# Opening of an attention with a scan beside it: the scan's kernels loaded in quarters and reordered on GpSimd, context chunks copied on the chip, the second unit's preparation not put ahead

## The chip, the cores and the metric

The kernel runs on 1 core of a Trainium2 chip. The metric is device time in microseconds of one execution; 3074.2 us is the median of 3 runs of the kernel before.

## The reference

Two layers of a transformer-like block over 1024 latent tokens and 256 context tokens, width 1024, all in fp32. Each layer first mixes tokens with four head groups that read one input projection and write one output projection, then applies a squared-ReLU MLP:

```
z  = modulate(rms_norm(x, g_pre_mix), sh1, sc1) @ w_in          # zc the same for the context
oa = gqa_mixer(z, zc, ...)     # A: grouped-query attention, 4 heads, 2 key heads, latent + context keys
ob = s5_mixer(z, zc, ...)      # B: bidirectional diagonal state-space scan, 16 groups x 16 channels, 64 states
on = na_mixer(z, zc, ...)      # C: 2-D neighbourhood attention, 4 heads
od = fourier_mixer(z, ...)     # D: 2-D DFT, then a linear map
y  = concatenate([oa, ob, on, od]) @ w_out
x  = x + g1 * rms_norm(y, g_post_mix)
x  = x + g2 * rms_norm(sq_relu_mlp(modulate(rms_norm(x, g_pre_mlp), sh2, sc2), w_mlp1, w_mlp2), g_post_mlp)
```

The context is carried through the first layer only (it is read but not updated in the second). For this change B matters: for each of 16 groups and both directions, a linear recurrence over 1280 positions, started for the latent part from the context's final states:

```
hc = linear_scan(einsum('blgh,gph->blgp', uc_g, bbar), abar, None, reverse)
h0 = hc[:, 0] if reverse else hc[:, -1]
h  = linear_scan(einsum('blgh,gph->blgp', u_g, bbar), abar, h0, reverse)
y  = y + einsum('blgp,ghp->blgh', h, cmat).real.reshape(b, n, S5_CH)
```

## The kernel before

The program is unrolled Python, run once, on one core. It goes layer by layer through stages: first norm, input projection, attention, output projection, MLP. Products that must be exact in fp32 are made of three products of a high and a low part. A planner, which works with a timing model when the program is built, takes what the Python code emits with its dependencies and gives each engine a fixed order: among instructions that it believes ready, the one emitted earliest goes first. An engine then runs its list strictly in order and waits in front of an instruction whose inputs are not there. What is emitted under `early(gen, n)` (L143) counts as emitted n instructions earlier. SP issues the loads and stores, in order as well.

The attention stage (`attention`, L827) works through units: with j one of two key heads and b a block of queries, first the grouped-query units (in layer 0: j0b0, j0b1, j0b2, j1b0, j1b1, j1b2, where b2 are the context's queries; in layer 1 without b2), then four heads of neighbourhood attention. Three streams run beside each other. The main of unit i (`gqa_main`, L629) goes through 10 key tiles in two steps each: scores on TensorE (L653), an exponential on ScalarE (L654), two steps later the products with the values (L622). The preparation of unit i+1 (`gqa_prep`, L555) is woven in three steps to one step of the main, under `early` with 600: the queries are split and transposed (L522, copies at L149), then come 16 reductions of score tiles (products L586, VectorE L588) and 4 of the context's (L593, L595), whose results are transposed into the second query tile. The preparation of unit 0 runs beside the end of the input projection. The scan (`s5_scan`, L1259) is the third stream, one step to two steps of the main.

The scan works in chunks of 8 positions: 128 chunks of latents and 32 of context, so that u, the tile s5u, holds for a partition (position in the chunk, channel) and each of 16 groups 192 columns: 32 context chunks, 128 latent chunks, and the context again, as the two directions need it. `s5_load` (L1250) fills it with 16 loads from HBM: for each of the 8 positions one of 160 columns (L1256) and one of the 32 context columns (L1257). The tile tm (s5tm) holds for each group the 128x128 matrix that carries the inside of a chunk. It comes from HBM as t0 (s5t), all 16 groups by 8 loads at once (L1334), and four times, behind group 1, 5, 9 and 13 in the code, four groups of it are reordered into tm by ScalarE (L1345, recorded at the helper's line L149). For each group, `front` (L1288) multiplies u by v (product L1290), rotates by cs and sn on VectorE with a swap of halves by ScalarE, scans, multiplies on GpSimd (L155), swaps again on ScalarE and adds on GpSimd; `rear` (L1318), two groups later, makes the output from tm (L1321) and from the scan's result (L1323) and stores it. The loads of v, cs and sn (L1284) are issued one group ahead, with two buffers.

Of the kernel before, what the change touches and what calls it, by code (L numbers as in the profile page):

```python
# [11 lines left out]
F32 = mybir.dt.float32  # L12
# [20 lines left out]
class K:  # L33
# [795 lines left out]
    def attention(self, l, st, o, fnet):  # L829


        units = st["units"]
        ng = sum(u["kind"] == "g" for u in units)
        ctx = any(u.get("b") == 2 for u in units)
        up = self.open(f"up{l}")
        for n, w, b in (("on", 512, 2), ("onn", TOK, 1), ("rt", 10, 2)):
            up.tile([128, w], F32, tag=n, bufs=b, name=n)
        pg = self.open(f"attG{l}")
        st["fp"], st["pg"] = up, pg
        pc = self.open(f"attC{l}", "right")  # L840
        st["k"].append(self.keys(pc, "g1"))
        st["q"].append(self.queries(pc, "g1", 1024))
        if ctx:
            st["q"].append(self.queries(pc, "gc", 512))
        sp = self.open(f"s5{l}")
        side, every = self.s5_scan(sp, l), 2
        self.ps_open("A", 2, "AM")
        for i, u in enumerate(units):
            ahead = [] if u.get("b") == 2 else [i + 1]
            if i + 1 < len(units) and units[i + 1].get("b") == 2:  # L850
                ahead.append(i + 2)
            ahead = [k for k in ahead if k < len(units)]
            if sp is not None and any(units[k]["kind"] == "n" for k in ahead):

                for _ in side:
                    pass
                sp.release()
                sp = None
                pn = st["pn"] = self.open(f"attN{l}")
                st["n"] = [self.na_set(pn, 0)]  # L860
            if i == ng:
                for p in (pc, st["pb"], st["zp"]):
                    p.release()
                pa = self.open(f"attO{l}")
                st["n"].append(self.na_set(pa, 1))
                self.ps_open("A", 2, "A")
                self.ps_open("M")
                side, every = fnet, 5 / 2
            main = self.gqa_main(st, u, o) if u["kind"] == "g" else self.na_main(st, u, o)
            main = self.along(main, st.get("fin", iter(())))  # L870
            main = self.every(main, side, every)
            self.weave(main, self.early(itertools.chain(*(self.attn_prep(st, k) for k in ahead)), 600), 3)
        for _ in st["fin"]:
            pass
        for _ in fnet:
            pass
        for p in (pa, pn, pg, up):
            p.release()
# [371 lines left out]
    def s5_load(self, u, l):  # L1250

        nc = self.nc
        us = self.u5D[l].rearrange("(g h) j c -> j h g c", h=16)
        for j in range(8):
            js = slice(j * 16, (j + 1) * 16)
            nc.sync.dma_start(u[js, :, 32:192], us[j])  # L1256
            nc.sync.dma_start(u[js, :, 0:32], us[j][:, :, 128:160])  # L1257

    def s5_scan(self, p, l):  # L1259

        nc = self.nc
        dr = self.s5D[l]
        u = p.tile([128, 16, 192], F32, name="s5u")
        self.s5_load(u, l)
        r8 = p.tile([128, 32], F32, name="r8")
        nc.sync.dma_start(r8, dr["r8"])
        tm = p.tile([128, 16, 128], F32, name="s5tm")

        def swap(dst, src):

            for a in (0, 64):
                self.copy(dst[a:a + 64], src[64 - a:128 - a])


        zs = [p.tile([128, 2, 160], F32, name=f"z{i}") for i in range(3)]
        for z in zs:
            nc.vector.memset(z[:, 0, 128:129], 0.0)
            nc.vector.memset(z[:, 1, 159:160], 0.0)

        def ins(g):  # L1280

            ts = [p.tile([128, 2, w], F32, tag=n, bufs=2, name=n) for n, w in (("v", 128), ("cs", 160), ("sn", 160))]
            for t, n in zip(ts, ("v", "cs", "sn")):
                nc.sync.dma_start(t, dr[n][:, g])  # L1284
            return ts

        def front(g, v, cs, sn):
            pv = self.ps1()[:, :320].rearrange("p (d c) -> p d c", d=2)  # L1288
            for d in range(2):
                nc.tensor.matmul(pv[:, d], v[:, d, :], u[:, g, 32 * d:32 * d + 160], start=True, stop=True)  # L1290
            m1, m2, m3 = (p.tile([128, 2, 160], F32, tag=n, bufs=2, name=n) for n in ("m1", "m2", "m3"))
            self.tt(m2, pv, sn, OP.mult)
            self.tt(m1, pv, cs, OP.mult)
            swap(m3, m2)
            self.tt(m1, m1, m3, OP.subtract)
            gg = p.tile([128, 2, 160], F32, tag="gg", bufs=2, name="gg")
            for d in range(2):
                y, x = gg[:, d, :], m1[:, d, :]
                if d:
                    y, x = y[:, ::-1], x[:, ::-1]  # L1300
                k = d * 16 + g
                nc.vector.tensor_tensor_scan(y, r8[:, k:k + 1].to_broadcast([128, 160]), x, 0.0, op0=OP.mult, op1=OP.add)
            z1, z2 = (p.tile([128, 2, 160], F32, tag=n, bufs=2, name=n) for n in ("g1", "g2"))
            self.tt(z1, gg, sn, OP.mult, nc.gpsimd)
            swap(z2, z1)
            self.tt(gg, gg, cs, OP.mult)
            z = zs[g % 3]

            for d, c0, c1, n in ((0, 0, 31, 128), (0, 129, 0, 31), (1, 0, 1, 159)):
                self.tt(z[:, d, c0:c0 + n], gg[:, d, c1:c1 + n], z2[:, d, c1:c1 + n], OP.add, nc.gpsimd)  # L1310
            return z

        def outs(g):

            x = p.tile([128, 2, 128], F32, tag="x1", bufs=2, name="x1")
            nc.sync.dma_start(x, dr["x"][:, g])
            return x

        def rear(g, z, x):
            py = self.ps1()[:, :160]  # L1320
            nc.tensor.matmul(py, tm[:, g, :], u[:, g, 32:192], start=True, stop=False)  # L1321
            for d in range(2):
                nc.tensor.matmul(py, x[:, d, :], z[:, d, :], start=False, stop=d == 1)  # L1323
            y = p.tile([128, 160], F32, tag="y", bufs=2, name="y")
            self.copy(y, py)
            nc.sync.dma_start(dr["y"][g], y)

        before, xs = [], []
        tabs = ins(0)
        yield  # L1330

        t0 = p.tile([128, 16, 128], F32, name="s5t0")
        for j in range(8):
            nc.sync.dma_start(t0[j * 16:(j + 1) * 16], dr["e"][:, :, (7 - j) * 16:(7 - j) * 16 + 128])  # L1334
        yield
        yield
        for g in range(16):
            now, tabs = tabs, ins(g + 1) if g < 15 else None
            st = (g, front(g, *now))
            if g < 2:  # L1340
                xs.append(outs(g))
            if g % 4 == 1:

                gs = slice(g - 1, g + 3)
                self.copy(tm[:, gs].rearrange("p g (h j) -> p g j h", j=8), t0[:, gs].rearrange("p g (j h) -> p g j h", j=8))  # L1345
            yield
            before.append(st)
            if len(before) > 2:
                rear(*before.pop(0), xs.pop(0))
                xs.append(outs(g))  # L1350
                yield
        for st in before:
            rear(*st, xs.pop(0))
            yield
# [490 lines left out]
```

## Time and profile before

| | |
|---|---|
| median of 3 runs (lowest, highest) | 3074.2 us (3071.66, 3086.07) |
| profiled execution | 3064.83 us |
| its span, first to last instruction | 3062.3 us |
| mean granted TensorE clock | 0.972 of full |
| busy: TensorE, VectorE, ScalarE, GpSimd | 2920.0, 1632.1, 1084.1, 901.7 us |
| first attention begins about, second about | 303 us, 1936 us |

All readings are of one profiled execution; times are from the start of its span. Instructions of the program's queues run in order on each engine, so an engine's idle time in front of an instruction names what it waited for. PE is TensorE, DVE VectorE, ACT ScalarE, POOL GpSimd, SPq the queue of SP that issues loads and stores. A shared helper has one line for all its uses: L149 is every copy by ScalarE, L155 every two-input operation, L522 every transpose of this kind.

### The profile page before, as it was taken

How to read it: one execution, taken by the hardware profiler on the slowest of the kernel's cores; microseconds unless marked ns; L12 is line 12 of the kernel's file. 1: busy time of each engine (PE TensorE's matmuls, PEld its weight loads, DVE VectorE, ACT ScalarE, POOL GpSimd, SP SyncE). 2: the span in 40 equal slices, each digit the busy share in tenths (PEclk: the TensorE clock that was granted, in tenths of full speed). 3: DMA queues.
4: the chain of work that ended last, by engine and by line, in shares of the span. 5: the costliest groups of instructions: out<-in, count | busy, mean ns of one | idle time of the engine just before them, and what ended most of it. 6: DMA issues, size and time to landing. Idle time of an engine off the chain costs nothing. (4 is left out here: it accounts for less than half of the span.)

```text
span 3062.3 us, 41885 instructions
## 1 busy us (share of the span) xinstructions
PE 2920.0 (95%) x16492; PEld 2539.9 (83%) x16492; DVE 1632.1 (53%) x2245; ACT 1084.1 (35%) x1858; POOL 901.7 (29%) x849
## 2 busy tenths in 40 slices
PE   6999899999999999999999899898999999999998
PEld 3798798887888889898988788798887888888887
DVE  3465565664775544754554776465755333343334
ACT  3444554553422222422222344365543322121212
POOL 1464123225421122512112564022224111111113
PEclk8999798999999999999999999899999999999999
DMA  7533525342543322532333443525343111111113
GB/s 271 185 117 113 89 80 137 113 145 99 174 140 128 128 82 83 171 112 97 117 104 104 160 122 123 78 81 154 108 145 124 43 54 56 42 49 48 56 42 110
DMA packets 237077, 335.36 MB, mean 110 GB/s; under 512 B 46705, under 2 KB 182993, under 8 KB 236881
## 3 DMA queue, kind: packets, MB, share of 16 engines
q1 hardware_dynamic: 236880, 332.70, 35.6%
q8 instruction: 129, 2.11, 0.3%
q14 instruction: 68, 0.55, 0.1%
HBM read 279.06 MB, written 53.54 MB: 109 GB/s over the span
## 5 line engine op out<-in xcount | busy, mean ns | idle before, releaser
L161 PE MATMUL ps<-mh,wh 128*128 128x320 f32 (+1 forms) x1536 | 518.8, 338 | 11.9 <-DVE y L155 6.8
L149 ACT ACTIVATE wh<-raw 128x1024 fp32r<-128x1024 f32 x234 | 243.0, 1057 | 791.2 <-PE ps L163 551.6
L163 PE MATMUL ps<-mh,wl 128*128 128x320 f32 (+1 forms) x1536 | 517.1, 337 | 0.6 <-DVE wl L152 0.6
L162 PE MATMUL ps<-ml,wh 128*128 128x320 f32 (+1 forms) x1536 | 516.9, 337 | 0.0
L161 PE MATMUL ps<-wh,hidh 128*128 128x512 f32 x1152 | 452.3, 393 | 2.2 <-DVE y L155 2.0
L163 PE MATMUL ps<-wh,hidl 128*128 128x512 f32 x1152 | 448.3, 390 | 3.1 <-POOL hidl L152 3.1
L162 PE MATMUL ps<-wl,hidh 128*128 128x512 f32 x1152 | 450.0, 391 | 0.0
L155 DVE TENSOR_TENSOR y<-ps,y 128x1024 f32<-128x1024 f32 (+1 forms) x253 | 306.7, 1218 | 262.1 <-PE ps L163 261.8
L152 POOL TENSOR_TENSOR hidl<-r,hidh 128x640 fp32r<-128x640 f32 (+1 forms) x128 | 189.1, 1477 | 675.6 <-DVE r L155 656.5
L152 DVE TENSOR_TENSOR wl<-raw,wh 128x1024 fp32r<-128x1024 f32 x188 | 286.2, 1532 | 170.7 <-ACT wh L149 163.8
L161 PEld LDWEIGHTS ps<-mh,wh 128*128 128x128 f32 x1536 | 289.8, 189 | 37.5 <-issue 7.3
L163 PEld LDWEIGHTS ps<-mh,wl 128*128 128x128 f32 x1536 | 289.5, 189 | 21.2 <-DVE wl L152 1.2
L162 PEld LDWEIGHTS ps<-ml,wh 128*128 128x128 f32 x1536 | 289.7, 189 | 20.9
L161 PEld LDWEIGHTS ps<-wh,hidh 128*128 128x128 f32 x1152 | 217.2, 189 | 53.7 <-issue 6.2
L163 PEld LDWEIGHTS ps<-wh,hidl 128*128 128x128 f32 x1152 | 216.9, 188 | 49.2 <-POOL hidl L152 3.5
L152 POOL TENSOR_TENSOR wl<-raw,wh 128x1024 fp32r<-128x1024 f32 x48 | 117.2, 2442 | 472.4 <-ACT wh L149 472.1
L162 PEld LDWEIGHTS ps<-wl,hidh 128*128 128x128 f32 x1152 | 217.1, 188 | 43.3
L155 DVE TENSOR_TENSOR r<-r 128x640 f32<-128x640 f32 (+1 forms) x128 | 98.9, 773 | 241.9 <-ACT hidh L1511 241.4
L1509 ACT ACTIVATE r<-ps 128x640 f32<-128x640 f32 (+1 forms) x128 | 82.3, 645 | 366.7 <-PE ps L163 359.9
L622 PEld LDWEIGHTS ps<-zg,e 128*128 128x128 f32 x1312 | 186.1, 199 | 15.8 <-ACT e L654 0.8
L622 PE MATMUL ps<-zg,e 128*128 128x65 f32 x1312 | 179.1, 273 | 0.4 <-ACT e L654 0.4
L294 DVE SCALAR_TENSOR_TENSOR acc<-raw,cst,acc 128x1024 f32<-128x1024 f32 x70 | 101.5, 1474 | 137.3 <-DMA raw<-in_w_ada_dram 137.3
(433 smaller groups left out, 5431.3 us busy)
## 6 DMA issues: line engine op xcount, KB each, us to landing
raw<-in_w_mlp_dram SPq DMA_DIRECT2D x192, 512.0 KB
raw<-in_w_ada_dram SPq DMA_DIRECT2D x96, 512.0 KB
raw<-in_w_in_dram SPq DMA_DIRECT2D x28, 512.0 KB
x<-x SPq DMA_DIRECT2D x26, 512.0 KB
x<-h SPq DMA_DIRECT2D x18, 512.0 KB
x<-in_x_dram SPq DMA_DIRECT2D x16, 512.0 KB
raw<-in_w_out_dram SPq DMA_DIRECT2D x16, 512.0 KB
bq<-in_na_bq_dram SPq DMA_DIRECT2D x8, 800.0 KB
```

Of the source, the lines that this page charges most:

```text
L149: self.nc.scalar.activation(out, in_, AF.Copy, scale=scale)
L152: (eng or self.nc.vector).tensor_tensor(out=out, in0=a, in1=b, op=OP.subtract)
L155: (eng or self.nc.vector).tensor_tensor(out=out, in0=a, in1=b, op=op)
L161: self.nc.tensor.matmul(ps, ah, bh, start=start and i == 0, stop=False)
L162: self.nc.tensor.matmul(ps, ah, bl, start=False, stop=False)
L163: self.nc.tensor.matmul(ps, al, bh, start=False, stop=stop and i == n - 1)
L294: nc.vector.scalar_tensor_tensor(acc[c], x, col, acc[c], op0=OP.mult, op1=OP.add)
L622: self.nc.tensor.matmul(po[:, b * 512 + c * 65:b * 512 + c * 65 + 65], e, vf[:, kt, :], start=False, stop=(b, c) in end)
L1509: nc.scalar.activation(r.rearrange("p (b n) -> p b n", b=nb), ps[:, :nb, :w], AF.Relu)
```

## The change

The context's second place in u is no longer loaded: after the 8 loads GpSimd copies columns 160 to 191 of all groups to columns 0 to 31. The tile t0 shrinks from 16 groups to 4, with two buffers. A new inner function `kernels(g0)` issues the 8 loads for four groups and lets GpSimd reorder them into tm; it is called behind the front of groups 0, 4, 8 and 12, where before all loads stood ahead of group 0 and ScalarE reordered behind groups 1, 5, 9 and 13. While unit 0 runs, the preparation of unit 1 counts as emitted 40 instructions earlier in place of 600; for all later units 600 stays.

```diff
-            self.weave(main, self.early(itertools.chain(*(self.attn_prep(st, k) for k in ahead)), 600), 3)
+            self.weave(main, self.early(itertools.chain(*(self.attn_prep(st, k) for k in ahead)), 600 if i else 40), 3)
...
             nc.sync.dma_start(u[js, :, 32:192], us[j])
-            nc.sync.dma_start(u[js, :, 0:32], us[j][:, :, 128:160])
+
+        nc.gpsimd.tensor_copy(u[:, :, 0:32], u[:, :, 160:192])
...
-        t0 = p.tile([128, 16, 128], F32, name="s5t0")
-        for j in range(8):
-            nc.sync.dma_start(t0[j * 16:(j + 1) * 16], dr["e"][:, :, (7 - j) * 16:(7 - j) * 16 + 128])
+        def kernels(g0):
+
+            t0 = p.tile([128, 4, 128], F32, tag="s5t0", bufs=2, name="s5t0")
+            gs = slice(g0, g0 + 4)
+            for j in range(8):
+                nc.sync.dma_start(t0[j * 16:(j + 1) * 16], dr["e"][:, gs, (7 - j) * 16:(7 - j) * 16 + 128])
+            nc.gpsimd.tensor_copy(tm[:, gs].rearrange("p g (h j) -> p g j h", j=8), t0.rearrange("p g (j h) -> p g j h", j=8))
+
...
-            if g % 4 == 1:
-
-                gs = slice(g - 1, g + 3)
-                self.copy(tm[:, gs].rearrange("p g (h j) -> p g j h", j=8), t0[:, gs].rearrange("p g (j h) -> p g j h", j=8))
+            if g % 4 == 0:
+                kernels(g)
```

## Rows read from the trace of the kernel before

**Rows 1.** The page's busy times: us, share of the span, instructions.
```profile
PE 2920.0 (95%) x16492; PEld 2539.9 (83%) x16492; DVE 1632.1 (53%) x2245; ACT 1084.1 (35%) x1858; POOL 901.7 (29%) x849
```
**Rows 2.** Stretches: length, busy us (instructions) by engine, clock, DMA share, GB/s.
```profile
326.70:334.40 7.70, 0.02 (x1) 0.00 (x0) 0.90 (x2) 4.31 (x6) 0.00 (x0) 0.64 0.64 117
334.40:342.60 8.20, 8.16 (x29) 7.20 (x30) 2.67 (x4) 1.74 (x4) 0.00 (x0) 0.51 0.01 2
...
350.00:470.00 120.00, 118.39 (x871) 109.45 (x871) 79.58 (x162) 79.33 (x165) 37.52 (x71) 1.00 0.28 81
...
1959.30:1969.40 10.10, 0.00 (x0) 0.00 (x0) 1.43 (x3) 4.30 (x6) 0.00 (x0) 0.72 0.59 99
1969.40:1976.60 7.20, 7.16 (x28) 6.68 (x29) 1.47 (x3) 1.67 (x3) 0.00 (x0) 0.50 0.00 0
```
**Rows 3.** Timeline, layer 0: start, us, engine, line, operation [idle before <-releaser].
```profile
330.09 3.87 ACT L149 ACTIVATE s5tm<-s5t 128x512 f32<-128x512 f32 x4 [10.63 <-DMA cs<-s5cs]
...
334.44 1.22 PE L653 MATMUL ps<-g0q,g0k 128*128 128x512 f32 x2 [7.72 <-ACT e L654]
```
**Rows 4.** Timeline, layer 1, the same place.
```profile
1965.10 3.87 ACT L149 ACTIVATE s5tm<-s5t 128x512 f32<-128x512 f32 x4 [10.43 <-DMA v<-s5v]
...
1969.44 1.22 PE L653 MATMUL ps<-g0q,g0k 128*128 128x512 f32 x2 [10.16 <-ACT e L654]
```
**Rows 5.** Stretches around the openings and at the change of attention, columns as before.
```profile
304.00:314.00 10.00, 7.22 (x27) 4.28 (x26) 7.89 (x14) 1.62 (x3) 2.32 (x2) 0.72 1.22 148
314.00:326.00 12.00, 11.54 (x42) 9.33 (x41) 5.29 (x9) 4.28 (x7) 0.00 (x0) 0.53 1.23 140
...
326.00:328.00 2.00, 0.72 (x4) 0.37 (x3) 1.29 (x2) 0.00 (x0) 0.00 (x0) 1.00 1.23 129
...
470.00:560.00 90.00, 82.01 (x552) 74.40 (x551) 52.55 (x106) 42.81 (x83) 26.25 (x27) 0.89 0.66 165
...
2090.00:2180.00 90.00, 81.36 (x564) 72.93 (x563) 53.09 (x109) 42.46 (x81) 26.98 (x32) 0.92 0.61 156
```
**Rows 6.** Groups by form: busy us, mean ns | idle before. GpSimd's, then ScalarE's.
```profile
L182 POOL CAST wh<-raw 128x1024 fp32r<-128x1024 f32 x2 | 2.1, 1037 | 25.8 <-DMA raw<-in_w_out_dram 25.8
...
L152 POOL TENSOR_TENSOR wl<-tab,wh 128x512 fp32r<-128x512 f32 x4 | 5.2, 1288 | 15.2 <-ACT wh L149 15.2
...
L149 ACT ACTIVATE g1q<-ps 128x512 fp32r<-128x512 f32 x8 | 4.6, 599 | 3.9 <-DMA uf<-cst__3248 3.5 <-PE ps L522 0.3
L149 ACT ACTIVATE s5tm<-s5t 128x512 f32<-128x512 f32 x4 | 3.9, 1120 | 10.6 <-DMA cs<-s5cs 10.6
```
**Rows 7.** Timeline, layer 0: the scan's first work on TensorE and on GpSimd.
```profile
349.36 0.76 PE L1290 MATMUL ps<-s5u,v 128*128 128x160 f32 x4
...
353.30 0.88 POOL L155 TENSOR_TENSOR g<-gg,sn 128x320 f32<-128x320 f32 x1 [43.10 <-DVE ql L155]
...
358.67 0.49 PE L1321 MATMUL ps<-s5u,s5tm 128*128 128x160 f32 x2
```
**Rows 8.** SP's queue, layer 0: issues in order of time, then its longest wait.
```profile
311.25 0.34 SPq L1257 DMA_DIRECT2D s5u<-u  x1
...
313.09 0.33 SPq L1257 DMA_DIRECT2D s5u<-u  x1
...
318.42 5.29 SPq L1334 DMA_DIRECT2D s5t<-s5e  x8
...
SPq L1284 <- PE ps L593: 22.1, 1, 22.1
```
**Rows 9.** The second unit: reductions (ns min/median/max), last query copies, first scores, longest wait.
```profile
L588 DVE TENSOR_REDUCE nm<-ps x61: 658/685/693, 292.3 to 440.3; 128x1 f32<-128x512 f32 x61
...
355.68 1.08 ACT L149 ACTIVATE g1q<-ps 128x512 fp32r<-128x512 f32 x2
...
367.79 0.71 PE L653 MATMUL ps<-g1q,g0k 128*128 128x512 f32 x2
...
373.92 0.73 PE L653 MATMUL ps<-g1q,g0k 128*128 128x512 f32 x2 [1.47 <-ACT e L654]
```

## The prediction

> **What bounds the kernel now.** I read the page's busy times and slices first, then a table of stretches, then the engines in order of time where TensorE stood still, then the queue of SP. The profiled execution took 3064.8 us, of which 3062.3 are the span; the median of the three runs shown is 3074.2, so it lies 9.4 us below, and I carry its differences over to the median.
>
> TensorE is busy 95% of the span, so the idle 5% (some 142 us) and the stretches at a low clock are all that a reordering can win [rows 1]. Two of its gaps lie just behind the opening of the two attentions, and in both its busy time is practically zero: 326.7 to 334.4 and 1959.3 to 1969.4 us [rows 2]. Behind them attention is bound by TensorE: from 350 to 470 us it works 118.4 of 120 us at full clock while VectorE and ScalarE have 80 each [rows 2].
>
> What ends the gap is read in order of time. In the first layer ScalarE stands idle for 10.63 us, from 319.5, does four copies s5tm<-s5t in one go, and only then the next exponentials; TensorE goes on at 334.44, released by an exponential after 7.72 us of idling [rows 3]. The second layer repeats it: 10.43 us of waiting, the same four copies, 10.16 us of idle TensorE [rows 4]. The trace names the cs or v load as releaser; those loads stand behind the s5t load in SP's queue, and the copies' only input is s5t, so I take the wait as that on the s5t load (all 16 groups, 1 MB) landing. ScalarE works strictly in order, so the next exponentials stand behind copies that nobody needs for long: the first product with s5tm comes at 358.67 [rows 7].
>
> The gap costs twice. TensorE's clock is at half (the 0.50 level, 1.2 GHz) in 334.4 to 342.6 and in 1969.4 to 1976.6 [rows 2], so what ran there took double. Before the first gap the clock had come back to full (1.00 in 326 to 328 [rows 5]), so it is the gap that threw it down again.
>
> **The change, part by part.**
>
> *Reorder off ScalarE.* The four copies of 1120 ns per layer leave ScalarE, and with them its wait for the load. What goes: 7.72 us in the first layer and 10.16 in the second. Without the gap the clock stays up, and 8.2 us and 7.2 us of half-clock work would take half: 4.1 and 3.6 us. Sum 7.7 + 10.2 + 4.1 + 3.6 = 25.6 us. The bounds: nothing, if another wait takes its place; 25.6 plus the small idle pieces just before (0.46 of 12 us in 314 to 326 [rows 5], taken for both layers), 26.5. Next late would be the exponentials themselves, which follow at TensorE's pace. I take all of 25.6, since TensorE stays the busiest engine behind it and what starts earlier there ends earlier.
>
> *The reorder on GpSimd.* Five new instructions a layer: four reorders and one plain copy, each 128x512. The trace has no such reorder on GpSimd. Below: half the 1037 ns of its plain 128x1024 conversion, 0.52 us. Above: its two-input 128x512, 1.29 us. On ScalarE the reorder costs 1120 against 599 ns for a plain copy of that size [rows 6]; that ratio on 0.52 gives 0.97, and I take 1.0. Five microseconds a layer are hidden while GpSimd does nothing: its first scan multiply at 353.30 comes after 43 us of idleness [rows 7]. Should the cover go, a late multiply holds the swaps on ScalarE and behind them the exponentials. The Trainium skill (GPSIMD Engine Reference, Performance pitfalls for Q7 kernels) gives 1.9 cycles an element, 2.9 for wide strides on the read; at its 1.2 GHz an estimate of 0.8 to 1.2 us, inside these bounds, so the sum stays; no run here has shown it yet.
>
> *Context chunks copied on the chip.* Eight loads of 32 KB a layer go, in runs of 128 bytes (32 values). SP issues one pair of loads, 192 KB, each 1.84 us there (from 311.25 to 313.09 [rows 8], and so in the pairs before). If bytes set the pace, the pair without its sixth takes 1.53; if packets do, half, 0.92. The eight end 2.4 to 7.3 us earlier. The copy needs the last of the eight loads, as the first product on s5u did, and adds 0.5 to 1.3 us. That product runs at 349.36, some 36 us after the last load was issued [rows 7, 8], or some 24 with the 11.8 us of the first layer gone: worth nothing by itself, costs nothing. The Trainium skill (DMA: Bandwidth & Descriptors, Specifications) states 512 bytes as the least transfer at line rate; by it the 7.3 is nearer. The rows only bracket it; it moves the second rival, not the sum.
>
> *The load in quarters.* 32 issues in place of 8, less the 8 chunk loads: 16 more a layer on SP. Eight whole ones took 5.29 us to issue, 0.66 each [rows 8], an upper bound; the cheapest there took 0.33: 5 to 11 us. Two buffers make the third quarter wait for the first reorder; behind it stand the next groups' v, cs and sn loads. SP has cover: it then waited 22.1 us for TensorE [rows 8]. Cost 0; if the cover is gone, some of the 11 us reach the third group's products, behind which there is other work for TensorE.
>
> *Second unit not put ahead.* Its 20 reductions (0.69 each, 13.8 us on VectorE) were done before its last query copies, which end at 356.8, and its first scores began at 367.79: 11 us of slack [rows 9]. Interleaved three steps to one of the first unit, its 23 steps are traced by the 8th of some 21, so they keep most of it. At that boundary TensorE idled 1.47 us [rows 9]. I charge as much again per layer, 3.0 us; bounds 0 and the 23.4 us a layer of the third rival.
>
> Sum: -25.6 + 3.0 = -22.6 us: 3042.2 on the profiled execution, 3051.6 on the median, so **3052**. Its own range is 3044 to 3059 (26.5 won and a little luck; 15.4 left). With 0.5% (15.4 us) as what a measurement tells from no change, that is faster.
>
> **Rivals.**
> 1. *Forecast*: both gaps go, about -22. Chance 0.55.
> 2. *The wait moves.* The planner that fixed each engine's order put the copies where it believed the load landed, some 10 us before it did. It can do so again: the first scan product drawn into TensorE's waits of 304 to 314 (7.2 of 10 us busy [rows 5]) and standing there for the chunk copy; or GpSimd standing before a quarter, the scan multiply behind it, then swaps and exponentials. For: GpSimd, idle, invites it, and the last s5u load, issued at 313.09 [rows 8], moves only to 306 to 311 and lands later. Against: a quarter lands before the whole, and higher-priority work stood before the scan. Price: 4 to 10 us back per layer, so -22.6 + 8 to 20: 3060 to 3072, middle 3066, mostly no change. Chance 0.23.
> 3. *The second unit is late (slower).* At the first boundary TensorE waits for the whole preparation: 13.8 us of reductions, two query copies of 0.6 [rows 6], and a clock like that behind the first unit's own preparation, 0.72 for 10 and 0.53 for 12 us [rows 5], which is 8.4 us lost: 23.4 a layer, 47 in all, less the 25.6, +21: 3095. It decides from 12.8 us a layer, that is from about half of that left over at the boundary. For: the third unit's preparation keeps its 600 and now ranks before it. Against: the slack above, and that unit's queries go into the buffer which the first unit still reads. Chance 0.12.
> 4. *More than the sum.* The scan's earlier start also fills the weak stretch at the change to the second kind of attention (82.0 of 90 us busy in 470 to 560, 81.4 in 2090 to 2180 [rows 5]); half of those 16.6 us: -31, 3043. Chance 0.10.
>
> That the change does nothing of what it says is in the second, with the wait merely on another engine.
>
> **How the numbers follow.** Faster by over 0.5%: most of the forecast (0.49), all of the fourth (0.10), a little of the second (0.03): 0.62. Slower: most of the third, 0.10, and 0.02 of the second: 0.12. Same: 0.26. The range leaves out the third and the tail of the fourth: 3036 to 3078.
>
> **What would show it.** Right: no ScalarE copies s5tm; exponentials following each other with under 4 us between them from 317 and 1946 on; no TensorE gap over 2 us until the first boundary; full clock from about 326 and 1951 on; the reorders on GpSimd at about 1 us. Wrong: TensorE waiting before L1290 or GpSimd's multiplies waiting on DMA (second), a gap and half clock at the first scores of the second unit (third), or attention shorter by 25 us and the time lost again behind it.

## The result, and the profile after

The changed kernel takes 3041.24 us (median of 5 executions, 3037.68 to 3051.14), against 3074.2 us before (3063.73 to 3086.07): a ratio of 0.9891, 95% interval [0.9862, 0.9919], 33 us. It is faster, as forecast; the forecast was 3052 us with a range of its own from 3044 to 3059, so the median lies 3 us under that. The profiled execution took 3037.68 us, 3035.5 of them the span.

The page's busy times, in the columns of [rows 1]: the work has hardly changed, TensorE's share of a shorter span has risen.

```profile
PE 2916.6 (96%) x16492; PEld 2538.7 (84%) x16492; DVE 1635.7 (54%) x2245; ACT 1078.5 (36%) x1850; POOL 912.6 (30%) x859
```

Stretches of the kernel after, in the columns of [rows 2]: the places of the two former gaps, the stretch from 350 us on, the boundary to the second unit, and the second layer's opening.

```profile
320.00:330.00 10.00, 10.00 (x39) 8.38 (x39) 4.97 (x8) 3.70 (x6) 1.73 (x2) 0.56 0.57 150
330.00:340.00 10.00, 10.00 (x70) 9.15 (x70) 5.85 (x9) 3.45 (x6) 3.49 (x3) 1.00 0.24 51
350.00:470.00 120.00, 117.97 (x833) 108.61 (x832) 74.05 (x148) 75.75 (x157) 35.79 (x67) 0.96 0.28 81
366.30:376.50 10.20, 10.20 (x48) 8.98 (x47) 0.82 (x1) 6.10 (x12) 0.56 (x2) 0.50 0.02 7
1940.00:1950.00 10.00, 10.00 (x69) 9.11 (x69) 5.75 (x9) 3.25 (x6) 1.68 (x2) 1.00 0.51 137
1950.00:1960.00 10.00, 10.00 (x75) 9.35 (x74) 7.54 (x14) 4.27 (x8) 4.22 (x4) 1.00 0.32 67
```

Both openings are now without a gap: 20.00 busy of 20.00 us in each, where TensorE had stood for 7.72 and 10.16 us [rows 3, 4]. The clock is full from 328.7 to 366.3 us, and in the second opening from 1939.8 us on; the 0.96 of the long stretch is the half clock of the fourth row. GpSimd's timeline in the first opening shows who does the waiting now (columns of [rows 3]):

```profile
320.37 0.61 POOL L1258 COPY s5u<-s5u 128x512 f32<-128x512 f32 x1 [4.88 <-PE ps L586]
325.85 1.12 POOL L1339 COPY s5tm<-s5t 128x512 f32<-128x512 f32 x1 [4.87 <-DMA s5t<-s5e]
330.11 1.13 POOL L1339 COPY s5tm<-s5t 128x512 f32<-128x512 f32 x1 [3.13 <-DMA s5t<-s5e]
...
338.27 1.19 POOL L1339 COPY s5tm<-s5t 128x512 f32<-128x512 f32 x1 [2.59 <-DMA s5t<-s5e]
344.85 0.87 POOL L155 TENSOR_TENSOR g<-gg,sn 128x320 f32<-128x320 f32 x1 [5.38 <-DVE ql L155]
```

The waits on s5t have not gone: GpSimd stands in front of each quarter, 2.59 to 4.87 us, and still idles 5.38 us before its first scan multiply. ScalarE's exponentials in the same stretch wait for nothing but TensorE:

```profile
320.83 1.08 ACT L654 ACTIVATE e<-ps 128x512 f32<-128x512 f32 x2
...
329.27 0.60 ACT L654 ACTIVATE e<-ps 128x512 f32<-128x512 f32 x1 [3.37 <-PE ps L653]
```

**Where the time went.** I cut both spans at the same products: end of the first layer's input projection, last values product of grouped-query attention, first w_out product, end of the first MLP, and so on. First before, then after; the rows are grouped-query part, neighbourhood part, output projection with MLP (all first layer), then grouped-query and neighbourhood part of the second layer.

```profile
303.20:504.70 201.50, 185.28 (x1235) 166.49 (x1234) 115.93 (x232) 110.16 (x214) 47.02 (x80) 0.91 0.45 96
504.70:647.10 142.40, 133.81 (x968) 122.07 (x968) 101.11 (x243) 82.55 (x187) 36.11 (x46) 0.94 0.40 114
647.10:1712.10 1065.00, 1040.94 (x5680) 921.80 (x5680) 589.73 (x471) 302.29 (x373) 309.78 (x203) 0.99 0.37 123
1935.90:2118.60 182.70, 167.19 (x1143) 151.91 (x1141) 103.44 (x208) 101.90 (x195) 49.09 (x79) 0.93 0.48 105
2118.60:2252.00 133.40, 121.76 (x852) 108.31 (x852) 93.43 (x223) 72.67 (x163) 29.27 (x45) 0.93 0.39 114
```

```profile
307.60:498.70 191.10, 182.98 (x1239) 164.62 (x1237) 116.20 (x232) 107.24 (x210) 51.97 (x85) 0.94 0.40 100
498.70:646.80 148.10, 139.35 (x969) 126.69 (x967) 102.53 (x243) 82.46 (x187) 35.48 (x46) 0.91 0.37 109
646.80:1704.80 1058.00, 1038.61 (x5680) 921.50 (x5680) 589.37 (x471) 302.73 (x373) 310.02 (x203) 0.99 0.38 124
1927.10:2095.80 168.70, 163.19 (x1148) 148.15 (x1146) 104.52 (x207) 98.80 (x191) 54.48 (x84) 0.98 0.46 113
2095.80:2225.70 129.90, 117.91 (x853) 106.53 (x853) 95.01 (x225) 72.51 (x163) 30.78 (x44) 0.94 0.40 117
```

The two grouped-query parts, where the gaps lay, are shorter by 10.4 and 14.0 us, together 24.4. TensorE's idle time there (length less busy) fell from 16.2 to 8.1 and from 15.5 to 5.5 us, 18.1 together. The first layer's output projection and MLP, whose code is untouched, gave 7.0 more, the second neighbourhood part 3.5. The first neighbourhood part took 5.7 more than before, and the code before the first attention, untouched too, 4.4 more.

For all profiled executions of this study I split the span further: TensorE's idle time; the clock's part (over the recorded intervals of granted clock, the time that TensorE was busy times the share of the clock not granted); and the rest, which is work at full clock. The other rows are the experiments below. The five columns on the left are the lengths of the parts just named, the three on the right are sums over the whole span, all in us:

```
                        query1 neigh1 out+MLP1 query2 neigh2 |  idle clock   work
before                   201.5  142.4   1065.0  182.7  133.4 | 142.3  61.0 2859.0
after                    191.1  148.1   1058.0  168.7  129.9 | 119.0  61.5 2855.1
after, again             190.6  155.3   1057.4  171.2  131.3 | 120.9  67.7 2853.2
GpSimd + 40              193.8  141.4   1057.7  172.7  131.2 | 116.9  57.1 2857.1
after, on ScalarE        195.7  142.3   1058.3  176.5  131.0 | 121.2  59.8 2857.5
GpSimd alone             184.1  156.0   1064.3  169.4  145.3 | 126.8  72.2 2857.3
GpSimd alone, again      191.7  142.6   1064.4  171.0  154.7 | 128.1  78.7 2856.8
after, with 600          187.1  155.9   1062.5  167.1  144.2 | 131.0  67.5 2856.5
quarters alone           198.1  146.6   1064.7  175.2  144.9 | 133.8  76.6 2855.0
GpSimd + 40 in layer 1   192.1  163.1   1059.7  169.5  151.4 | 126.4  93.5 2854.7
GpSimd + 40 in layer 2   183.1  148.4   1064.5  170.7  138.2 | 125.3  59.8 2855.8
after, 40 everywhere     187.2  146.0   1062.3  169.3  140.6 | 122.3  61.9 2858.8
chunk copy alone         205.4  162.7   1060.0  182.3  129.1 | 144.5  77.4 2856.7
40 alone                 202.5  145.0   1056.7  193.4  152.1 | 142.1  92.5 2855.3
```

The work is the same within 6 us in all fourteen; what differs is idle time and clock. A ratio below comes from 5 rounds with the kernel before on the same chip, 6 to 12 executions of the kernel that is tried. The table has one execution each, and some lie far from the median of their kernel: that of "GpSimd + 40 in layer 1" 20 us above it, those of "in layer 2", "after, on ScalarE" and "GpSimd + 40" 16 to 19 us below.

### The profile page after: what moved, and what is told of

Same layout as the page of the kernel before. It is cut to its first block, busy times and chain, and to the rows that moved or that the text cites. A ratio compares the mean times of both kernels' runs of the same rounds, so it can differ in the third digit from the quotient of the medians.

```text
span 3035.5 us, 41960 instructions
## 1 busy us (share of the span) xinstructions
PE 2916.6 (96%) x16492; PEld 2538.7 (84%) x16492; DVE 1635.7 (54%) x2245; ACT 1078.5 (36%) x1850; POOL 912.6 (30%) x859
```

## The experiments

My theory after the result: (A) the two gaps give the forecast's 22 us, and the rest of the 33 is clock elsewhere. The rivals: one of the small edits (chunk copy, 40) carries part of it; or the quarters do, and not the engine.

**The reorder alone on GpSimd** (kernel before; load whole, 600 and chunk loads kept).

```diff
-                self.copy(tm[:, gs].rearrange("p g (h j) -> p g j h", j=8), t0[:, gs].rearrange("p g (j h) -> p g j h", j=8))
+                nc.gpsimd.tensor_copy(tm[:, gs].rearrange("p g (h j) -> p g j h", j=8), t0[:, gs].rearrange("p g (j h) -> p g j h", j=8))
```

> The kernel before with one edit: the four reorders a layer go from ScalarE to GpSimd; the kernels are still loaded whole, the chunk loads stay, the second unit stays put ahead. Theory A (the gap is ScalarE standing in order in front of the load): no TensorE gap over 2 us behind the opening, the stage from the end of the input projection to the last grouped-query product takes about 191 and 169 us as in the changed kernel (before 201.5 and 182.7), the whole about 22 us under the kernel before. Rival B (the backlog of small loads is the cost): the gap shrinks by less than half, the whole within 8 us. Rival C (the wait moves to GpSimd, which stands for the whole load, and the scan behind it): TensorE waits before the scan's products, the whole 5 to 15 us under the kernel before.

Ratio 0.9941 [0.9913, 0.9969], 3061.36 us. The largest wait of TensorE is 0.47 us in the first opening and 1.40 us in the second. GpSimd now stands 21.18 us in front of the whole load, and its first scan multiply still has 2.51 us to spare (TensorE's timeline, then GpSimd's):

```profile
319.68 0.73 PE L653 MATMUL ps<-g0q,g0k 128*128 128x512 f32 x2 [0.47 <-ACT e L654]
...
333.20 4.15 POOL L1345 COPY s5tm<-s5t 128x512 f32<-128x512 f32 x4 [21.18 <-DMA x<-s5x]
...
339.86 0.87 POOL L155 TENSOR_TENSOR g<-gg,sn 128x320 f32<-128x320 f32 x1 [2.51 <-DVE ql L155]
```

The query parts are 184.1 and 169.4 us, against 191.1 and 168.7 in the changed kernel. This edit alone removes both gaps. But about half of the changed kernel's gain is missing: the two neighbourhood parts take 156.0 and 145.3 us (142.4 and 133.4 before), with a low clock.

**The chunk copy alone.**

```diff
-            nc.sync.dma_start(u[js, :, 0:32], us[j][:, :, 128:160])
+        nc.gpsimd.tensor_copy(u[:, :, 0:32], u[:, :, 160:192])
```

> The kernel before with one edit: the eight chunk loads a layer are replaced by one copy on GpSimd; ScalarE still reorders all kernels after one whole load. Theory A: ScalarE waits less, since the load lands 2.4 to 7.3 us earlier, but still does its four copies in one go: gaps of 1 to 8 us in place of 7.7 and 10.2, the whole 5 to 15 us under the kernel before. Rival B (the backlog is the cost): gaps below 1 us and all of some 22 us.

Ratio 1.0004 [0.9976, 1.0031]: worth nothing, as the prediction had it; the 5 to 15 us that I expected for this run did not come. The gap stays; TensorE's timeline has it at another product and longer, 13.08 us (10.85 us in the second layer):

```profile
330.30 2.87 PE L586 MATMUL ps<-g0k,g1q 128*128 128x512 f32 x5 [13.08 <-ACT g1q L149]
```

**40 in place of 600 alone.**

```diff
-            self.weave(main, self.early(itertools.chain(*(self.attn_prep(st, k) for k in ahead)), 600), 3)
+            self.weave(main, self.early(itertools.chain(*(self.attn_prep(st, k) for k in ahead)), 600 if i else 40), 3)
```

> The kernel before with one edit: while unit 0 runs, the preparation of unit 1 counts as emitted 40 instructions earlier in place of 600. Theory A: ScalarE still stands in front of the load, gaps of 7 to 11 us stay, the whole within 6 us of the kernel before. Rival D (the second unit's preparation put ahead is what holds the first unit): both gaps go or halve, 10 to 22 us won.

Ratio 1.0007 [0.9977, 1.0037]. Both gaps stay (TensorE's timeline, first and second layer):

```profile
339.92 1.22 PE L653 MATMUL ps<-g0q,g0k 128*128 128x512 f32 x2 [9.30 <-ACT e L654]
...
1966.22 1.22 PE L653 MATMUL ps<-g0q,g0k 128*128 128x512 f32 x2 [12.93 <-ACT e L654]
```

The sum is nothing, but the parts of the profiled execution differ: output projection and MLP are 8.3 us shorter than before, the second layer's query and neighbourhood parts 10.7 and 18.7 us longer.

**The changed kernel with 600 again.**

```diff
-..., 600 if i else 40), 3)
+..., 600), 3)
```

> The changed kernel without its first edit: quarters, reorder on GpSimd and chunk copy, with the second unit put 600 ahead as before. Theory A: the same as the changed kernel within 5 us, stage lengths about 191 and 169 us, no gap behind the opening. Rival D: some 10 to 20 us slower than the changed kernel.

Ratio 0.9944 [0.9914, 0.9973], like the reorder alone, and the written order of TensorE's instructions is the same as there. Quarters and chunk copy add nothing to the reorder. The version is slower than the changed kernel, as rival D expected and not theory A: the 40, which alone gave nothing, now looked like 16 us. The next four runs, on one chip, were to settle that.

**The changed kernel again.** No edit.

> The changed kernel once more, unaltered, beside the others on one chip. Theory A (the two gaps are worth some 22 us, the rest of the 33 measured first was the clock in stretches that the change does not touch): ratio to the kernel before 0.990 to 0.995, so 3048 to 3063 where before takes 3078, the same as the version with 600 put back and the version with the reorder alone. Theory B (not putting the second unit ahead is worth some 10 to 16 us more once the gap is gone): ratio 0.987 to 0.991, 3038 to 3050, and outside the interval of the version with 600.

Ratio 0.9883 [0.9852, 0.9914], 3049.63 against 3083.07 us. Theory B, not A.

**Reorder on GpSimd and 40, nothing else.** The first and the third diff above.

> The kernel before with two edits only: the four reorders on GpSimd, and the second unit not put ahead (40 for 600); load whole, chunk loads kept. Theory B: like the changed kernel, ratio 0.987 to 0.991. Theory A: like the reorder alone, ratio about 0.994, within its interval 0.991 to 0.997. A third theory (the quarters are what makes the changed kernel faster than the reorder alone) also expects 0.994 here.

Ratio 0.9884 [0.9854, 0.9915]. These two edits are the whole gain; TensorE's order is that of the changed kernel, instruction by instruction.

**The reorder alone, again.** No edit against the first experiment.

> The kernel before with the reorder alone on GpSimd once more, same instructions as in the first run of it. If the half-clock stretches in the neighbourhood part (17.8 to 38.3 us of its first stage, 3.2 to 40.7 of its second) belong to the kernel's order of instructions, they stand at the same places again; if they come from execution to execution by chance, one or both are elsewhere or gone and the stage is 8 to 15 us shorter. Time: ratio 0.991 to 0.997 again.

Ratio 0.9962 [0.9938, 0.9986], 3072.03 us on the chip on which the changed kernel took 3049.63: 22 us apart, the intervals do not touch. The long half clock in the second neighbourhood part is there again (154.7 us), that in the first is not (142.6 for 156.0). So the first comes and goes from execution to execution; the second was there in all three profiled executions with this order (145.3, 154.7 and, with quarters and chunk copy, 144.2 us). How it goes, in stretches of the second neighbourhood part, reorder alone first, then the changed kernel (its repeat):

```profile
2101.50:2113.90 12.40, 8.11 (x31) 6.65 (x31) 4.06 (x11) 0.86 (x3) 0.24 (x2) 0.50 0.94 245
2114.00:2124.00 10.00, 10.00 (x39) 9.29 (x39) 8.23 (x18) 6.51 (x16) 2.84 (x4) 0.50 0.09 30
2124.00:2134.00 10.00, 10.00 (x45) 9.71 (x44) 4.55 (x9) 3.94 (x10) 1.11 (x4) 0.50 0.16 53
2134.00:2139.10 5.10, 5.10 (x23) 4.81 (x23) 3.12 (x7) 1.82 (x4) 3.00 (x5) 0.50 0.17 52
2139.10:2150.00 10.90, 10.90 (x96) 10.00 (x95) 6.76 (x17) 5.11 (x12) 3.79 (x7) 1.00 0.45 143
```

```profile
2103.30:2112.50 9.20, 6.49 (x27) 5.48 (x27) 3.83 (x9) 0.93 (x3) 0.24 (x2) 0.50 0.95 242
2112.60:2117.00 4.40, 4.39 (x16) 4.17 (x17) 2.73 (x6) 3.02 (x6) 0.00 (x0) 0.51 0.68 189
2117.00:2130.00 13.00, 12.87 (x99) 11.98 (x99) 12.30 (x30) 7.42 (x17) 4.36 (x8) 1.00 0.19 57
```

Both fall to half while TensorE waits at the change of attention. The changed kernel is back at full clock 4.4 us after its last wait, the reorder alone only after 25.1 us, in which TensorE was busy without a break. What stands in front, reorder alone and then the repeat:

```profile
2113.31 0.63 ACT L149 ACTIVATE uh<-u 128x512 fp32r<-128x512 f32 x1 [9.41 <-DMA u<-uf]
...
2113.99 0.48 PE L161 MATMUL ps<-csh,uh 128*128 128x128 f32 x1 [2.29 <-ACT uh L149]
```

```profile
2112.61 1.19 PE L778 MATMUL ps<-n0q,n0k 128*128 128x512 f32 x2 [1.80 <-DMA n0q<-nmt]
2113.47 1.08 ACT L782 ACTIVATE e<-ps 128x512 f32<-128x512 f32 x2 [1.97 <-PE ps L778]
```

In the reorder alone ScalarE stands 9.41 us in front of a conversion whose load (Fourier's u) has not landed, and the neighbourhood's exponentials stand behind it: an order of the same kind as the one removed, at another place. In the changed kernel the planner wrote the exponentials first. In waiting this costs TensorE little (2.29 us against 1.80); whether it is what holds the clock down is not shown.

**The changed kernel with the four reorders back on ScalarE.**

```diff
-            nc.gpsimd.tensor_copy(tm[:, gs]...)
+            self.copy(tm[:, gs]...)
```

> The changed kernel with its four reorders a layer given back to ScalarE, everything else kept (quarters, chunk copy, 40). Theory A (ScalarE, in order, stood before the load): ScalarE stands before the first quarter; that lands earlier than the whole did, so the gap on TensorE is 0 to 5 us per layer in place of 7.7 and 10.2, and two more copies wait for a buffer; ratio 0.995 to 1.000. Rival (the quarters alone remove the gap, the engine does not matter): no gap over 2 us in either opening, ratio 0.987 to 0.994.

Ratio 0.9902 [0.9878, 0.9927], 3057.81 us: in the rival's range and not in my theory's, though one gap is over the 2 us that the rival allows. ScalarE now waits for each quarter, but between two waits come exponentials; TensorE's largest gaps (first and second layer) are

```profile
331.15 0.73 PE L653 MATMUL ps<-g0q,g0k 128*128 128x512 f32 x2 [1.26 <-ACT e L654]
...
1940.79 1.22 PE L653 MATMUL ps<-g0q,g0k 128*128 128x512 f32 x2 [3.65 <-ACT e L654]
```

The engine is not the only cure. Against the changed kernel's repeat the two query parts are 5.1 and 5.3 us longer; in the medians it is 8 us, and the intervals overlap.

**40 in the first layer only, then in the second only** (both with the reorder on GpSimd).

```diff
-..., 600 if i else 40), 3)
+..., 600 if i or l else 40), 3)
...
+..., 40 if l and not i else 600), 3)
```

> The reorder on GpSimd as in the reorder-alone kernel, and 40 for 600 in the first layer only. Theory C (the extra gain of the 40 has two places: the order of w_out and the start of the first MLP, some 7 us, belongs to the first layer's edit; the half clock at the start of the second layer's neighbourhood part, some 14 to 23 us, to the second layer's): w_out and MLP of the first layer 120.5 and 937.5 us together with a second neighbourhood part of 145 to 155 us; ratio 0.992 to 0.994. Rival D (the orders of both layers hang together, and the first layer's edit is what moves both): that part 130 us too, ratio 0.988.

> The reorder on GpSimd, and 40 for 600 in the second layer only. Theory C: second neighbourhood part 130 us, w_out and MLP of the first layer 122 and 942 as in the kernel before; ratio 0.989 to 0.992. Rival D: second neighbourhood part 145 to 155, ratio 0.994 to 0.996, as the reorder alone.

Ratios 0.9942 [0.9913, 0.9971] and 0.9941 [0.9909, 0.9972], neither clear of the reorder alone (0.9941 and 0.9962). First the second neighbourhood part of the run with 40 in the first layer, its long stretch of half clock, and a row of ScalarE's timeline there; then output projection with MLP and second neighbourhood part of the run with 40 in the second layer:

```profile
2114.10:2265.50 151.40, 136.45 (x852) 122.89 (x852) 96.89 (x224) 72.60 (x163) 29.48 (x45) 0.83 0.35 103
2126.00:2165.60 39.60, 39.60 (x163) 37.55 (x164) 20.30 (x45) 15.68 (x33) 9.17 (x15) 0.50 0.32 94
...
2126.82 1.08 ACT L782 ACTIVATE e<-ps 128x512 f32<-128x512 f32 x2 [3.45 <-PE ps L778]
```

```profile
635.50:1700.00 1064.50, 1041.82 (x5680) 923.47 (x5680) 592.12 (x471) 302.50 (x373) 307.24 (x203) 0.99 0.37 123
...
2093.30:2231.50 138.20, 122.09 (x852) 110.50 (x852) 93.66 (x224) 72.44 (x163) 29.57 (x44) 0.90 0.38 109
```

The first layer's edit shortens output projection and MLP (1059.7) and leaves a slow second neighbourhood part, as theory C said; but its profiled execution lies 20 us above the median, and the exponentials come first there, with ScalarE waiting for TensorE alone. The second layer's edit does the reverse only by half: 138.2 where C expected 130, at a ratio that rival D expected. TensorE's order in that part is one of its own in each of the two. The order of the second attention hangs on both edits; C holds for the first place and is not shown for the second.

**40 at every unit.**

```diff
-..., 600 if i else 40), 3)
+..., 40), 3)
```

> The changed kernel with 40 in place of 600 at every unit, not only the first: a try at a faster one. If what the 40 gives comes from preparation that stands in the way at its planned place, more of it goes: ratio under 0.985. If the later boundaries need their preparation ahead, TensorE waits there for reductions and query copies, 5 to 10 us a boundary at six or more boundaries, and the clock falls behind each: ratio 1.00 to 1.03. I lean to the second.

Ratio 0.9893 [0.9851, 0.9935]: neither expectation. The boundaries that I feared cost nothing (query parts 187.2 and 169.3 us), and nothing more is won; the second neighbourhood part is 140.6.

**The quarters alone** (ScalarE, chunk loads, 600).

```diff
-        t0 = p.tile([128, 16, 128], F32, name="s5t0")
+        def kernels(g0):
+            t0 = p.tile([128, 4, 128], F32, tag="s5t0", bufs=2, name="s5t0")
...
+            self.copy(tm[:, gs]..., t0...)
...
-            if g % 4 == 1:
+            if g % 4 == 0:
+                kernels(g)
```

> The kernel before with the load in quarters alone: the reorders stay on ScalarE (one per quarter, in front of each group of four), chunk loads and 600 kept. If either of the two edits (the quarters, or the other engine) is enough by itself against the gap: no gap over 2 us in either opening, attention parts of 188 to 196 and 171 to 178 us in place of 201.6 and 182.7, and with 600 kept the half clock at the start of the second neighbourhood part (140 to 155 us); ratio 0.993 to 0.997. If the quarters need GpSimd to be worth anything (ScalarE late once more through its order): gaps of 3 us or more, parts as before, ratio 0.998 to 1.001.

Ratio 0.9964 [0.9935, 0.9993]. The largest gaps are

```profile
334.12 0.74 PE L653 MATMUL ps<-g0q,g0k 128*128 128x512 f32 x2 [1.61 <-ACT e L654]
...
1960.63 1.19 PE L653 MATMUL ps<-g0q,g0k 128*128 128x512 f32 x2 [2.65 <-ACT e L654]
```

2.65 us is more than I had allowed, and 198.1 us in the first query part is 2 above the range; the ratio and the slow second neighbourhood part (144.9) are as expected. The quarters alone take most of the gap away, by letting exponentials pass between the waits.

No version beats the changed kernel beyond the measurement; with 0.9884 the two edits alone (GpSimd and 40) equal it with less code.

## Why the prediction was right, and where it was not

**The gap's removal: right, the clock term partly by luck.** Forecast 7.72 + 10.16 = 17.9 us of idling; the two query parts lost 18.1 in the profiled pair. Forecast 7.7 us of clock; the split has 13.9 before and 11.2 after in the first layer, 8.3 and 2.9 in the second: 8.1. Work there rose by 1.9, which leaves the 24.4 measured, against 25.6 forecast for this term. The idle time repeats: 7.7 to 9.1 and 5.3 to 7.7 us in the nine executions with the reorder on GpSimd. The clock does not: the same nine lose 2.6 to 13.9 us to it in the first query part and 1.6 to 4.7 in the second, so a pair that comes out at 8.1 is in part luck. The full clock came at 328.7 and 1939.8 us, where I had written about 326 and 1951.

**The reorder on GpSimd: right, a little low.** 1.12 to 1.31 us for 1.0 taken; the upper one is just over my bound of 1.29. The plain copy took 0.61. From the Trainium skill (GPSIMD Engine Reference, Performance pitfalls for Q7 kernels) I had an estimate of 0.8 to 1.2 us; the reorder lies at its upper end and above, the plain copy below. The page's dearer figure is for wide strides on the read, while this reorder reads t0 in order and has its stride on the write, so the page does not explain the price. Nothing hung on it: the scan multiply waited for VectorE.

**The wait moves (second rival): half right, without a price.** GpSimd does stand in front of every quarter. But its first multiply still had 5.38 us to spare (2.51 with the load whole), and no first scan product was held.

**Second unit not put ahead: the step that was mis-sized.** I charged 3.0 us. At the boundary to the second unit TensorE waits 1.48 us after, as 1.47 before [rows 9]:

```profile
365.86 0.89 PE L653 MATMUL ps<-g1q,g0k 128*128 128x512 f32 x2 [1.48 <-ACT e L654]
```

After it the clock was at half for 10.2 us, 5.1 us lost; but the repeat has no such stretch there, and the reorder alone with 600 has it in one of its two executions. With each first query part's clock loss taken out, it is 179.2 to 180.6 us in the nine executions with the reorder on GpSimd, 40 or 600. So the edit costs nothing at the boundary, and the third rival's 23 us a layer did not come. What I did not look for is that the edit changes the planner's order far behind the first unit. With the gap gone it is worth 0.8% (0.9883 and 0.9884 against 0.9962 on one chip; 0.6% against the 0.9941 and 0.9944 of another), in two places of the profiles. One is output projection and MLP of the first layer. TensorE's order there is that of the changed kernel in six of the fourteen executions, which take 1056.7 to 1059.7 us, and that of the kernel before in seven, which take 1062.3 to 1065.0: 6.0 us in the mean, with or without a gap at the opening. For this the forecast had no term. The other is the second neighbourhood part, 129.9 to 131.3 us in the four executions with the changed kernel's order against 144.2 to 154.7 in the four with that of the reorder alone, 16.4 in the mean. But the kernel before took only 133.4 us there, with 600, and the chunk copy alone 129.1: in the profiled executions the 40 mostly gives back there what the reorder with 600 had made worse.

**The fourth rival (more than the sum)** came nearest in time (3043), by a wrong reason: the weak stretches at the change of attention were not filled. The repeat still waits 4.36 and 1.80 us there.

**So why 33 and not 22?** The profiled pair differs by 26.8 us of span: 24.4 in the query parts, 7.0 in the first layer's output projection and MLP, 3.5 in the second neighbourhood part and 2.0 elsewhere, less the 5.7 and 4.4 named above. Against the forecast's 22.6, the 3.0 that I charged for the second unit were not due, and the 7.0 of output projection and MLP were missing. What more the medians show cannot be located: the profiled execution of the kernel before lay 9 us under its median, that of the changed one 4 under its own. Executions of one kernel scatter by the clock: the reorder alone took 3094.21 us at a mean granted clock of 0.960 and 3060.15 at 0.970.

**What stays open.** What at the second layer's change of attention decides whether the clock comes back after 4 or after 25 us. In the six executions in which ScalarE stands 7.5 to 9.9 us in front of Fourier's u there, one stretch of half clock lasts 23.9 to 37.6 us; in the four with the changed kernel's order 13.6 or 13.7. TensorE's order differs between the two groups as well, so they cannot tell which of the two it is. And neither is enough: with 40 in the first layer only, the exponentials come first and the half clock lasts 47.8 us all the same, in an execution 20 us above its kernel's median. Nor does TensorE's own idle time decide it: after its first wait there it idles 1.2 us with the 40 alone and 3.1 with the reorder alone, and the half clock lasts 34.1 and 37.6 us. I did not try that load by itself.

## What to carry to other kernels

A strictly ordered engine that feeds the busiest one should not be given work whose load may land late: move that work to an idle engine, or cut it so that feeding work passes between the waits; here the first took the gaps away and the second most of them. A planner's priority that changes nothing in the total while a larger gap stands can be worth most of a percent when that gap is gone, here in part because it gives back what the other edit lost elsewhere. So edits are tested together and apart, and looked at far behind the place where they are made. Split the span into idle time, clock and work before explaining a difference: here the work was the same within 6 us in every version.

## What the runs showed of the hardware

TensorE busy without a break does not by itself bring the clock back: 25.1 us at 0.50, from 2114.0 to 2139.1 us of the reorder alone, and 39.6 us from 2126.0 to 2165.6 us of the run with 40 in the first layer only. The Trainium skill (TensorE: Matmul & The Clock Gate, What's actually happening) says that the clock is throttled by default and activity releases it; busy time as the profile counts it was not enough for that here. And the same written order of TensorE's instructions takes different times, mostly by the clock: the first neighbourhood part has one order in thirteen of the fourteen executions (all but that with 40 everywhere), and took 141.4 to 163.1 us, of which 8 to 30 were clock.
